# A decoder layer with three branches on one core: memory weights split two halves ahead, sums of x a step ahead, and three queue orders changed

## The chip, the core and the metric

The kernel runs on one core of a Trainium2 chip. Five engines work side by side, each on its own queue of instructions: TensorE (PE in the profile; PEld is its loading of the stationary operand), VectorE (DVE), ScalarE (ACT), GpSimd (POOL) and SyncE (SP). Here SP only issues DMAs, and its queue takes them in order: an issue that has to wait holds everything behind it. GpSimd issues a few DMAs too.

The metric is the device time of one execution in microseconds (us). A profiled execution also has a span, from its first to its last recorded instruction.

## The reference

One step of a decoder layer with 1024 prompt tokens and 8 sample tokens, width 1024, all in float32:

```python
mkv = mem_prompt @ w_mem_kv                 # 256 memory tokens, 2 x 1024 columns
mk, mv = mkv[:, :, 0], mkv[:, :, 1]         # memory keys and values, both outputs too
z = x @ w_in                                # xr, yr, q, k, v, xq, gates
a_out = rg_lru(causal_conv(xr)) * gelu(yr)  # branch a
s_out = sliding_window_attention(q, k, v)   # branch s, window 128
c_out = mem_attn(xq, mk, mv)                # branch c
merged = sum(gates[n] * (br @ w_branch[n]) for n, br in enumerate((a_out, s_out, c_out)))
h = layer_norm(ALPHA * x + merged @ w_out)
gt, up = split(h @ w_gate_up)
y = layer_norm(ALPHA * h + (silu(gt) * up) @ w_down)
```

For the sample tokens the kernel also returns the two window caches, shifted by one row and with the new row at the end (`s_win_k`, `s_win_v`; in the kernel `o_swk`, `o_swv`).

## The kernel before

**Products.** Every matrix product is made of float32 operands that are split in two: `split` (L71) has ScalarE cast a tile to fp32r (the high part, L73) and VectorE subtract that from the source (the low part, L74). A product of two split tiles is three TensorE instructions, high by high, high by low, low by high (`mm3`, L107 to L109). In the names of the trace `_h`, `H` or a leading `h` is a high part, `_l`, `L` or `l` a low part.

**Weights.** `half_raw` (L82, load L84) brings half a block of weights, 128 x 512, into one of six staging buffers by a DMA on SP; `half_pair` (L87) gives its split parts one of five buffers for the high and four for the low part. `weights` (L91) does both for a whole block.

**Stages**, in order of time:
- `mem_kv` (L360): the keys and the values of the 256 memory tokens. `memT`, the memory, comes in four halves (`mem_raw`, `mem_split`). Eight key blocks `m` follow, each of two weight halves with 12 matmuls; then four value groups `h` of four halves with 12 matmuls each. `put` (L366) evicts a finished block from PSUM with a ScalarE copy (L368) into one of two staging buffers (`kvraw`) and stores it twice by GpSimd DMAs, as an output and as scratch for branch c.
- `project` (L265): z = x @ w_in, in 30 units. A unit is two blocks of 128 columns, computed by a scheme of seven products of half size instead of eight (`fast_step`, steps 0 to 6, 24 matmuls each). It needs seven sums and differences of quarters of x (`combos`, L157; VectorE makes them at L177, L180, L181 and L190 and each is split; there are 14, for seven steps and two halves `p` of the tokens) and seven of each unit's weights (`fast_quarter`, sums at L205). PSUM tiles of a unit are called `ub`, `ud`, `uc`; `u2s` is an eviction of `ub` (L246). A unit ends in `Finish.done` (L1175), which for the twelve gate units stores the two results `za` and `zb` into scratch `scr_g` (L1181).
- The attention of branch c over the memory and of branch s over the window, with the projections of branch a (`branch(0, "a")`) and c filled in between. `load_branch` (L118) brings a branch's input back from scratch: eight loads (L124) per chunk of tokens, into the tiles that later hold the low parts (`baL`), and splits them. `dec_win_scores` (L824) handles the window attention of the sample tokens, and at L834 issues two copies inside DRAM, from `cwk` and `cwv` to `o_swk` and `o_swv` (127 rows for each of 8 tokens).
- The output product and `ffn` (L1053): 22 blocks `f`, for each the weights `wfg` and `wfu` and per chunk of tokens two products `fg` and `fu`, the multiplication of the two (L1064) and the split of the result `gH`; between them the products `d` with `wdn`.

**What sets the order.** The instructions are written down once, for all engines. For `mem_kv` and the first six steps (`FIRST`) of the first unit `tc.manual_schedule` (L290) keeps the written order on SP, ScalarE, VectorE and TensorE. [...] `tc.issue_after(x)` and `add_manual_dep` put an instruction behind another in that order without a wait on the chip.

In `mem_kv` before, the order inside one key block is: for each half the split of that half, the load of the same half of the next block, 12 products; then a load of a quarter of x, for four of the blocks one step of `moving` (the `combos` generator), and the eviction of this very block. A value group loads and splits each half directly ahead of its products. `moving` makes a sum and splits it in the same step. After `mem_kv` come the loads of unit 0, three quarters of its weights, and per step of the first six one quarter and two steps of `moving`.

## Time and profile before

| what | value |
|---|---|
| median of three runs | 2045.55 us (2042.29 to 2048.28) |
| profiled execution | 2043.52 us, its span 2041.8 us |
| granted TensorE clock, mean | 0.988 |
| TensorE busy | 1974.8 us, 97% of the span |
| VectorE busy | 1199.2 us, 59% |
| ScalarE busy | 876.0 us, 43% |
| GpSimd busy | 126.1 us, 6% |
| DMA | 239.62 MB, 117 GB/s in the mean |

How to read it: the profile cuts the span in 40 slices and gives each engine's busy share in tenths (9 is 90% or more). A row of a single instruction has its start in us, its duration in us, engine, line of the kernel, operation, the tiles it writes and reads, shapes and types, and in brackets the idle time ahead of it with what ended that. A row of the waits names the group that waited, what released it, the total of the wait in us, the number of waits and the longest. A group's row has its line, engine, operation, tiles, count, then minimum, median and maximum in ns and the stretch in which it lies. A row of DMAs has the number of transfers, KB of each and the median us from issue to landing; an issuing row has the duration on the queue. The clock is the share of full speed that TensorE was granted.

### The profile page before, as it was taken

The numbers are of one execution on the slowest core, as the hardware profiler recorded it, in microseconds if no ns is written. First come the engines' busy times: TensorE is split into PE (matmuls) and PEld (weight loads), VectorE is DVE, ScalarE is ACT, GpSimd is POOL, SyncE is SP. The second block draws the span as 40 slices with busy tenths as digits, with TensorE's granted clock in tenths as the row PEclk, the third lists the DMA queues.
The fourth block names the chain that finished last, engine by engine and source line by source line (L and its number), as shares of the span: only waits on it lengthen the run. The fifth ranks groups of instructions, "written<-read, shape, count | busy, mean of one in ns | idle before, by whom it ended". The sixth has DMA issues, their size and how long they took to land.

```text
span 2041.8 us, 35429 instructions
## 1 busy us (share of the span) xinstructions
PE 1974.8 (97%) x13732; PEld 1937.0 (95%) x13732; DVE 1199.2 (59%) x2561; ACT 876.0 (43%) x1914; POOL 126.1 (6%) x192
## 2 busy tenths in 40 slices
PE   6799999999999988999999999999999999999997
PEld 5799999999999987988999999999999999999996
DVE  5678888977766654378876558623322232223357
ACT  4446655564655544378774244422111221122224
POOL 1200001010000000011110002100000000000001
PEclk9899999999999998999999999999999999999999
DMA  7455554546223366667525241111111111111112
GB/s 274 145 171 169 188 174 157 166 148 225 103 94 126 121 233 207 206 169 208 162 81 174 83 150 38 37 46 42 52 52 42 42 50 46 51 52 42 52 32 83
DMA packets 140824, 239.62 MB, mean 117 GB/s; under 512 B 17664, under 2 KB 67920, under 8 KB 140624
## 3 DMA queue, kind: packets, MB, share of 16 engines
q1 hardware_dynamic: 139120, 233.17, 35.6%
q0 software_dynamic: 1536, 4.20, 0.6%
q8 instruction: 108, 1.77, 0.4%
q14 instruction: 60, 0.49, 0.1%
HBM read 182.05 MB, written 57.33 MB: 117 GB/s over the span
## 4 chain that ended last, share of the span: by engine, by line
PE 87%; DVE 4%; ACT 4%; DMA 3%; issue 1%; SPq 0%; ACTq 0%; POOL 0%; DVEq 0%; POOLq 0%
PE ub L223 5%; PE ub L222 5%; PE ub L221 5%; PE fg L107 4%; PE fg L108 4%; PE fg L109 4%; PE fu L109 4%; PE fu L107 4%; PE fu L108 4%; PE d L107 3%; PE d L109 3%; PE d L108 3%; PE ud L223 3%; PE ud L222 3%; PE ud L221 3%; PE brs L107 1%
## 5 line engine op out<-in xcount | busy, mean ns | idle before, releaser
L107 PE MATMUL fg<-hH,wfg_h 128*128 128x384 f32 (+1 forms) x528 | 168.2, 319 | 2.9 <-DVE acc L1035 1.7
L108 PE MATMUL fg<-hL,wfg_h 128*128 128x384 f32 (+1 forms) x528 | 167.7, 318 | 0.4 <-DVE hL L1046 0.4
L109 PE MATMUL fu<-hH,wfu_l 128*128 128x384 f32 (+1 forms) x528 | 167.7, 318 | 0.0
L108 PE MATMUL fu<-hL,wfu_h 128*128 128x384 f32 (+1 forms) x528 | 167.6, 317 | 0.0
L107 PE MATMUL fu<-hH,wfu_h 128*128 128x384 f32 (+1 forms) x528 | 167.5, 318 | 0.0
L109 PE MATMUL fg<-hH,wfg_l 128*128 128x384 f32 (+1 forms) x528 | 167.5, 317 | 0.0
L1064 DVE TENSOR_TENSOR ft<-ft,fu 128x384 f32<-128x384 f32 (+1 forms) x66 | 33.8, 513 | 139.2 <-PE fu L109 139.1
L107 PE MATMUL d<-gH,wd_h 128*128 128x384 f32 (+1 forms) x360 | 114.4, 318 | 0.0
L108 PE MATMUL d<-gL,wd_h 128*128 128x384 f32 (+1 forms) x360 | 114.2, 317 | 0.0
L109 PE MATMUL d<-gH,wd_l 128*128 128x384 f32 (+1 forms) x360 | 114.2, 317 | 0.0
L1062 DVE SCALAR_TENSOR_TENSOR ft<-ft,fg 128x384 f32<-128x384 f32 (+1 forms) x66 | 33.8, 512 | 135.4 <-ACT ft L1061 133.2
L73 ACT CAST gH<-ft 128x384 fp32r<-128x384 f32 (+1 forms) x66 | 31.7, 480 | 174.8 <-DVE ft L1064 174.7
L107 PEld LDWEIGHTS fg<-hH,wfg_h 128*128 128x128 f32 x528 | 99.1, 188 | 3.9 <-DVE acc L1035 2.0
L108 PEld LDWEIGHTS fg<-hL,wfg_h 128*128 128x128 f32 x528 | 99.2, 188 | 1.0 <-DVE hL L1046 0.9
L109 PEld LDWEIGHTS fg<-hH,wfg_l 128*128 128x128 f32 x528 | 99.2, 188 | 0.0
L109 PEld LDWEIGHTS fu<-hH,wfu_l 128*128 128x128 f32 x528 | 99.2, 188 | 0.0
L107 PEld LDWEIGHTS fu<-hH,wfu_h 128*128 128x128 f32 x528 | 99.2, 188 | 0.0
L108 PEld LDWEIGHTS fu<-hL,wfu_h 128*128 128x128 f32 x528 | 99.1, 188 | 0.0
L1084 DVE SCALAR_TENSOR_TENSOR acc<-d,acc 128x384 f32<-128x384 f32 (+1 forms) x48 | 24.8, 516 | 108.4 <-PE d L109 108.4
L1061 ACT ACTIVATE ft<-fg 128x384 f32<-128x384 f32 (+1 forms) x66 | 30.1, 456 | 135.1 <-PE fg L109 135.1
L221 PE MATMUL ub<-th,u_4h 128*128 128x258 f32 x240 | 68.7, 286 | 5.8 <-ACT u2s L246 5.8
L556 ACT ACTIVATE bp<-bp,bst 128x257 f32<-128x257 f32 (+1 forms) x128 | 62.8, 493 | 18.8 <-DVE bst L552 18.6
(937 smaller groups left out, 6885.7 us busy)
## 6 DMA issues: line engine op xcount, KB each, us to landing
ur<-win SPq DMA_DIRECT2D x120, 256.0 KB, 2.8
dck<-cmk SPq DMA_DIRECT2D x32, 256.0 KB, 2.9
dcv<-cmvT SPq DMA_DIRECT2D x32, 256.0 KB, 3.1
st<-scr_q SPq DMA_DIRECT2D x32, 256.0 KB, 4.4
scr_g<-za SPq DMA_DIRECT2D x12, 516.0 KB, 2.8
scr_g<-zb SPq DMA_DIRECT2D x12, 516.0 KB, 3.9
x<-xQ SPq DMA_DIRECT2D x8, 516.0 KB, 6.0
scr_a<-ge SPq DMA_DIRECT2D x8, 516.0 KB, 2.8
```

The lines of the kernel that those rows point to most:

```text
L73: ins = self.nc.scalar.copy(hi, src).ins
L107: nc.tensor.matmul(ps, sh, mh, start=opens and i == 0, stop=False)
L108: nc.tensor.matmul(ps, sh, ml, start=False, stop=False)
L109: self.last_mm = nc.tensor.matmul(ps, sl, mh, start=False, stop=closes and i == last).ins
L221: mm(sh[:, w], xh, start=opens and k == 0, stop=False)
L222: mm(sh[:, w], xl, start=False, stop=False)
L223: self.last_mm = mm(sl[:, w], xh, start=False, stop=k == 3).ins
L556: nc.scalar.activation(x, x, AF.Exp, bias=st[:, g:g + 1], scale=-1.0, accum_out=st[:, 4 + g:5 + g])
L1061: nc.scalar.activation(t, pg, AF.Tanh, scale=0.5)
L1062: nc.vector.scalar_tensor_tensor(t, t, 1.0, pg, op0=ALU.add, op1=ALU.mult)
L1064: nc.vector.tensor_mul(t, t, pu)
L1084: nc.vector.scalar_tensor_tensor(a, ps, 0.5, a, op0=ALU.mult, op1=ALU.add)
```

## The change

- **Memory stage.** The 16 key halves and 16 value halves become one loop over 32 halves `n`. The load of a half is issued four halves ahead of its products (`fetch`), its split two halves ahead (`cut`), and the eviction of a finished block or group comes one half after its last product, in the next block's time. 24 matmuls on a constant tile (`WARM`) are put ahead of everything on TensorE. The loads of unit 0 and its first quarters are issued in the loop's last iterations.
- **Sums of x.** `combos` makes the sum for the next step ahead of the split for this one, and yields the number of VectorE operations; the memory loop takes a step whenever its count `due` allows one. The first six steps take two steps of `moving` each for k < 3 and one after that.
- **Branch a.** The eight loads of its first chunk depend, in order alone, on `last_gate`, the store of the last gate unit's `zb`: that store is queued behind them.
- **Cache copies.** The two copies inside DRAM move from `dec_win_scores` to the FFN, behind the weight loads of the blocks f = 2 and f = 4.

```diff
+WARM = 24
...
-            self.nc.sync.dma_start(lo.bitcast(F32), self.scr[br][:, k, t0:t0 + n])
+            ins = self.nc.sync.dma_start(lo.bitcast(F32), self.scr[br][:, k, t0:t0 + n]).ins
+            if br == "a" and c == 0:
+                self.tc.add_manual_dep(self.last_gate, ins.name, mybir.DependencyInfo(
+                    mybir.DependencyClass.NoSync, mybir.DependencyReason.DATA), reason="order of the queue")
...
-        for i in range(7):
-            for p in range(2):
-                b11, b12, b22, b21 = (xs.get((f, p)) for f in ((0, 0), (0, 1), (1, 1), (1, 0)))
-                if i == 0:
-                    keep(0, p, b11)
-                elif i == 1:
-                    t1 = self.zt(f"t1_{p}")
-                    tt(t1, b11, b12, ALU.subtract)
-                    keep(1, p, t1)
-                elif i == 2:
-                    tt(b12, b22, b12, ALU.subtract)
-                    tt(b11, b12, b11, ALU.add)
-                    keep(2, p, b11, -1.0)
-                elif i == 3:
-                    keep(3, p, b21)
-                elif i == 4:
-                    keep(4, p, b12)
-                elif i == 5:
-                    keep(5, p, b22)
-                else:
-                    tt(b11, b11, b21, ALU.subtract)
-                    keep(6, p, b11)
-                yield
+        def make(i, p):
+            b11, b12, b22, b21 = (xs.get((f, p)) for f in ((0, 0), (0, 1), (1, 1), (1, 0)))
+            if i == 1:
+                t1[p] = self.zt(f"t1_{p}")
+                tt(t1[p], b11, b12, ALU.subtract)
+                return 1
+            if i == 2:
+                tt(b12, b22, b12, ALU.subtract)
+                tt(b11, b12, b11, ALU.add)
+                return 2
+            if i == 6:
+                tt(b11, b11, b21, ALU.subtract)
+                return 1
+            return 0
+
+        steps = [(i, p) for i in range(7) for p in range(2)]
+        for n, (i, p) in enumerate(steps):
+            cost = 1
+            if n + 1 < len(steps):
+                cost += make(*steps[n + 1])
+            src = {0: xs[(0, 0), p], 1: t1.get(p), 2: xs[(0, 0), p], 3: xs.get(((1, 0), p)), 4: xs.get(((0, 1), p)),
+                   5: xs.get(((1, 1), p)), 6: xs[(0, 0), p]}[i]
+            keep(i, p, src, -1.0 if i == 2 else 1.0)
+            yield cost
...
-                self.mem_kv(moving, xs)
-            load(0)
-            for u, i in todo[:ahead]:
-                self.fast_quarter(st[u], i)
+                self.mem_kv(moving, xs, lambda: load(0), [lambda i=i: self.fast_quarter(st[0], i) for i in range(2)])
+            self.fast_quarter(st[0], 2)
             for k, (u, i) in enumerate(todo[:FIRST]):
                 if i == 1:
                     load(u + 1)
                 v, j = todo[k + ahead]
                 self.fast_quarter(st[v], j)
-                for _ in range(2):
+                for _ in range(2 if k < 3 else 1):
...
-            ps = self.bank("mm", f"mk{m}")[:, :NM]
-            for e in range(2):
-                hi, lo = self.half_pair(f"wmk{m}_{e}")
-                self.split(hi, lo, raws.pop((m, e)))
-                if m + 1 < KT:
-                    raws[m + 1, e] = key_half(m + 1, e)
-                for k in range(4 * e, 4 * e + 4):
-                    if k >= len(memx):
-                        mem_split(mraw[k // 2])
-                    w = slice(k % 4 * P, (k % 4 + 1) * P)
-                    self.mm3(ps, [((hi[:, w], lo[:, w]), memx[k])], k == 7, k == 0)
-            (f, th), p = quarters[m]
-            xs[(f, th), p] = self.x_quarter(f, th, p)
-            if m >= 2:
-                if m in (2, 3, 5, 7):
-                    next(moving)
-            put(ps, io["o_pmk"][:, m, :], "mk", m)
...
+        def fetch(n):
+            if n < 16:
+                src = io["wmk"][n // 2][:, n % 2 * h:(n % 2 + 1) * h]
+            else:
+                src = io["wmv"][(n - 16) // 2][:, n % 2 * h:(n % 2 + 1) * h]
+            raws[n] = self.half_raw(src, h, f"wm{n}r")
+
+        def cut(n):
+            pairs[n] = self.half_pair(f"wm{n}_")
+            self.split(*pairs[n], raws.pop(n))
+
+        def key(n):
+            m, e = n // 2, n % 2
+            if e == 0:
+                sums[m] = self.bank("mm", f"mk{m}")[:, :NM]
+            hi, lo = pairs.pop(n)
+            cols = [slice(i * P, (i + 1) * P) for i in range(4)]
+            self.mm3(sums[m], [((hi[:, w], lo[:, w]), memx[4 * e + i]) for i, w in enumerate(cols)], e == 1, e == 0)
+
+        def value(n):
+            g, j = (n - 16) // 4, n % 4
+            if j == 0:
+                sums[g] = [self.bank("mm", f"mv{g}_{tt}")[:, :256] for tt in range(2)]
+            hi, lo = pairs.pop(n)
+            cols = [slice(i * 256, (i + 1) * 256) for i in range(2)]
+            for tt in range(2):
+                xs_ = [tuple(a[:, tt * P:(tt + 1) * P] for a in memx[2 * j + i]) for i in range(2)]
+                self.mm3(sums[g][tt], [(x, (hi[:, w], lo[:, w])) for x, w in zip(xs_, cols)], j == 3, j == 0)
+
+        warm = self.bank("o", "warm")
+        for _ in range(WARM):
+            nc.tensor.matmul(warm[:, :P], self.ones, self.ones, start=True, stop=True)
+        for f in (partial(mem_raw, 0), partial(fetch, 0), partial(mem_raw, 1), partial(mem_raw, 2), partial(fetch, 1),
+                  partial(mem_raw, 3), partial(fetch, 2), partial(fetch, 3)):
+            f()
+        for f in (partial(mem_split, 0), partial(cut, 0), partial(mem_split, 1), partial(mem_split, 2), partial(cut, 1),
+                  partial(mem_split, 3)):
+            f()
+        due = -3.5
+        for n in range(32):
+            if n + 4 < 32:
+                fetch(n + 4)
+            elif n == 28:
+                load()
+            if n % 2 == 0 and n < 16:
+                (f, th), p = order[n // 2]
+                xs[(f, th), p] = self.x_quarter(f, th, p)
+            if n + 2 < 32:
+                cut(n + 2)
+            else:
+                quarters[n - 30]()
+            due += 0.6
+            if due > 0:
+                due -= next(moving)
+            (key if n < 16 else value)(n)
+            if 0 < n <= 16 and n % 2 == 0:
+                put(sums.pop(n // 2 - 1), io["o_pmk"][:, n // 2 - 1, :], "mk", n // 2 - 1)
+            if n > 16 and n % 4 == 0:
+                g = (n - 16) // 4 - 1
+                for tt, ps in enumerate(sums.pop(g)):
+                    put(ps, io["o_pmv"][:, tt, g * 256:(g + 1) * 256], "mv", 2 * g + tt)
+        for tt, ps in enumerate(sums.pop(3)):
+            put(ps, io["o_pmv"][:, tt, 768:], "mv", 6 + tt)
...
-        for name, cache, row in (("o_swk", "cwk", krow), ("o_swv", "cwv", self.vd)):
-            with self.tc.issue_after(self.last_load):
-                nc.sync.dma_start(io[name][:, 0:P - 1, :], io[cache][:, 1:P, :])
+        for name, row in (("o_swk", krow), ("o_swv", self.vd)):
...
+                if f in (2, 4):
+                    name, cache = (("o_swk", "cwk"), ("o_swv", "cwv"))[f // 2 - 1]
+                    with self.tc.issue_after(self.last_load):
+                        nc.sync.dma_start(io[name][:, 0:P - 1, :], io[cache][:, 1:P, :])
...
-                nc.sync.dma_start(b.scr["g"][:, 2 * j + e, :], z)
+                b.last_gate = nc.sync.dma_start(b.scr["g"][:, 2 * j + e, :], z).ins
```

More of the change, by code (lines that the diff above doesn't have):

```diff
@@ L160, in combos @@
         tt = self.nc.vector.tensor_tensor
+        t1 = {}
         def keep(i, p, src, sign=1.0):
@@ L358, in v_rows, with mem_kv @@
             yield
-    def mem_kv(self, moving, xs):
+    def mem_kv(self, moving, xs, load, quarters):
         nc, io = self.nc, self.io
-        memx = []
+        h = D // 2
+        memx, raws, pairs, sums = [], {}, {}, {}
+        order = [(f, p) for f in ((0, 0), (0, 1), (1, 1), (1, 0)) for p in range(2)]
         def put(ps, out, name, m):
@@ L379, in mem_split @@
             for i in range(2):
-                k = len(memx)
-                memx.append(tuple(self.ph.tile([P, NM], F32R, tag="mem", name=f"mem{e}{k}", bufs=16) for e in "hl"))
-                self.split(*memx[k], raw[:, i * NM:(i + 1) * NM])
-        quarters = [(f, p) for f in ((0, 0), (0, 1), (1, 1), (1, 0)) for p in range(2)]
-        raws = {}
-        mraw = [mem_raw(0)]
-        raws[0, 0] = key_half(0, 0)
-        mraw.append(mem_raw(1))
-        raws[0, 1] = key_half(0, 1)
-        mraw += [mem_raw(2), mem_raw(3)]
@@ L410, in mem_kv @@
-        for h in range(4):
-            pv = [self.bank("mm", f"mv{h}_{tt}")[:, :256] for tt in range(2)]
-            for j in range(4):
-                raw = self.half_raw(io["wmv"][2 * h + j // 2][:, (j % 2) * 512:(j % 2 + 1) * 512], 512, f"wmv{h}_{j}r")
-                wh, wl = self.half_pair(f"wmv{h}_{j}")
-                self.split(wh, wl, raw)
-                for tt in range(2):
-                    for i in range(2):
-                        xh, xl = (a[:, tt * P:(tt + 1) * P] for a in memx[2 * j + i])
-                        vh, vl = (a[:, i * 256:(i + 1) * 256] for a in (wh, wl))
-                        nc.tensor.matmul(pv[tt], xh, vh, start=j + i == 0, stop=False)
-                        nc.tensor.matmul(pv[tt], xh, vl, start=False, stop=False)
-                        self.last_mm = nc.tensor.matmul(pv[tt], xl, vh, start=False, stop=j + i == 4).ins
-                if j == 2 or (j == 1 and h >= 2):
-                    next(moving)
-            for tt, ps in enumerate(pv):
-                put(ps, io["o_pmv"][:, tt, h * 256:(h + 1) * 256], "mv", 2 * h + tt)
+                memx.append(tuple(self.ph.tile([P, NM], F32R, tag="mem", name=f"mem{e}{2 * k + i}", bufs=16)
+                                  for e in "hl"))
```

11 lines of the change are left out of this document (5 added, 6 removed).

## The prediction

> **What bounds the kernel now.** I read the page first, then the busy time by stretches, the waits of TensorE, the timelines of the stretches that stand out, and the DMA rates there.
>
> ```profile
> span 2041.8 us, 35429 instructions
> ```
> ```profile
> PE   6799999999999988999999999999999999999997
> ```
>
> The second line is TensorE's busy share in tenths, in 40 slices of 51 us. It is full nearly everywhere; it is not in the first two slices and has a dent at slices 15 and 16 (715 to 816 us). The FFN, 9s to the end, has nothing to give. A gain must come from those two places.
>
> ```profile
> 0.00:51.00 51.00, 34.29 (x229) 30.46 (x229) 25.80 (x39) 22.60 (x42) 9.02 (x20) 1.00 0.77 274
> 51.00:102.00 51.00, 38.73 (x262) 36.26 (x262) 33.54 (x55) 24.69 (x45) 10.27 (x24) 0.84 0.45 145
> 102.00:153.00 51.00, 51.00 (x419) 50.96 (x419) 40.57 (x106) 24.13 (x49) 0.92 (x2) 0.99 0.51 171
> ```
> ```profile
> PE mk L107 <- ACT wmk_0h L73: 12.7, 8, 5.6
> PE ub L221 <- ACT u2s L246: 5.8, 1, 5.8
> ```
>
> The columns of the first fence: stretch, its length, busy us of PE, PEld, DVE, ACT, POOL, clock, DMA share, GB/s. TensorE lacks 16.7 and 12.3 us there, and nothing from 102 us on. The waits name ScalarE: casts of the memory weights and evictions, although ScalarE is busy under half the time. So it is late by order, not by load:
>
> ```profile
> 15.58 0.28 PE L109 MATMUL mk<-memh,wmk_1l 128*128 128x256 f32 x1
> 15.90 0.37 ACT L368 COPY mkr<-mk 128x256 f32<-128x256 f32 x1 [3.16 <-PE mk L109]
> 16.17 0.62 ACT L73 CAST wmk_0h<-wmk_0r 128x512 fp32r<-128x512 f32 x1
> ```
> ```profile
> 33.14 1.06 ACT L73 CAST th<-t 128x1032 fp32r<-128x1032 f32 x1 [1.98 <-DVE t L177]
> ```
> ```profile
> L74 DVE TENSOR_TENSOR tl<-x,th x2: 1235/1235/1235, 18.3 to 22.9; 128x1032 fp32r<-128x1032 f32 x2
> L177 DVE TENSOR_TENSOR t<-x,x x2: 1224/1225/1226, 31.9 to 41.2; 128x1032 f32<-128x1032 f32 x2
> ```
>
> ScalarE's queue holds the eviction of a key block (15.90) ahead of the cast of the next block's weights (16.17). The eviction waits for TensorE's last product (15.58), TensorE for the cast: the eight blocks cost it the 12.7 us of the first wait. The cast of a sum (33.14) waits 1.98 us in the same queue for a sum that VectorE has just begun; a sum takes 1.22 us there and a split's low part 1.23 (min, median, max in ns).
>
> **The change, part by part.** *A, the memory stage and the first unit.* Cuts now stand two half blocks ahead and the eviction one iteration behind, so the eviction finds its product done and two cut halves lie between TensorE and a stall. What TensorE alone needs:
>
> ```profile
> 5.65 0.58 PE L107 MATMUL mk<-memh,wmk_0h 128*128 128x256 f32 x1 [5.65 <-ACT wmk_0h L73]
> ```
> ```profile
> 45.67 0.28 PE L422 MATMUL mv<-wmv_0h,meml 128*128 128x256 f32 x1
> ```
> ```profile
> 49.52 0.28 PE L422 MATMUL mv<-wmv_2h,meml 128*128 128x256 f32 x1
> ```
> ```profile
> 104.30 0.28 PE L221 MATMUL ud<-th,u_5h 128*128 128x258 f32 x1
> ```
>
> 33 steps from 45.67 to 49.52 are 0.1167 us each; in the steady stretch above, 51.00 us for 419 products are 0.122. The 32 half blocks of 12 products take 44.8 us, steps 0 to 4 of the first unit (120 products) 14.6. From the first product at 5.65 step 5 (ud) could start at 65.1; it starts at 104.30. Bound: 39.2 us.
>
> The loads forbid part of that. Up to the twentieth weight half (n=19, issued behind the last quarter of x) the SP queue must bring 4 halves of mem and 20 of weights at 0.262 MB and 8 quarters of x at 0.528; about 8 blocks of stores (2 x 0.131 MB each) share the engines: 6.3 + 4.2 + 2.0 = 12.5 MB.
>
> ```profile
> x<-xQ SPq DMA_DIRECT2D x8, 516.0 KB, 6.0
> ```
> ```profile
> mem<-memT SPq DMA_DIRECT2D x4, 256.0 KB, 4.4
> o_pmk<-mkr POOLq DMA_DIRECT2D x8, 128.0 KB, 4.2
> ```
> ```profile
> 0.00:5.00 5.00, 0.00 (x0) 0.00 (x0) 0.54 (x4) 1.94 (x4) 0.19 (x4) 1.00 0.49 162
> 5.00:11.30 6.30, 5.64 (x24) 5.22 (x24) 4.03 (x10) 3.27 (x9) 0.00 (x0) 1.00 0.94 292
> 11.30:16.00 4.70, 3.37 (x24) 2.96 (x24) 1.29 (x2) 1.51 (x4) 1.31 (x2) 1.00 0.98 353
> 16.00:20.50 4.50, 3.38 (x24) 2.96 (x24) 2.53 (x3) 2.26 (x4) 1.07 (x2) 1.00 1.04 414
> 20.50:25.10 4.60, 3.37 (x24) 2.96 (x24) 2.53 (x3) 2.36 (x4) 1.07 (x2) 1.00 1.03 389
> ```
>
> Length times rate: 0.81, 1.84, 1.66, 1.86, 1.79, so 7.96 MB by 25.1 us, with the engines full (share 0.94 and more) from 5 us on even now. The last three full rows make 385 GB/s. The other 4.5 MB take 11.8 us: half 19 lands at 36.9 and is cut 1.1 us later, so its product starts at 38.0, where TensorE alone would be at 32.3. Behind it loads are light (a half per 0.7 us against 1.4 of products). There VectorE decides once: n=19 brings two sums and a split, 1.22 + 1.22 + 1.23 us, where a half leaves it 1.4, and the third cut ahead is late by some 1.2. Thirteen halves of 1.40 end at 57.4. The first unit has 14.6 us of products against some 12 of VectorE work (four splits 4.9, two sums 2.4, seven half as wide 4.3), part of it begun before; its 5.8 us wait (second wait above) came from sums made in line, now a step ahead, so I cost it at nothing; without that cover it is 5.8 again. Step 5 starts at 72.0: **A = -32.3**. Bounds: -39.2 if loads hold nothing back; if the rest flows at 292 GB/s, the second row's rate, 15.4 us in place of 11.8, and half of the 5.8 stays, -26.
>
> [...]
>
> The 24 warm-up products (ones by ones, 128 wide) sit on an empty TensorE ahead of 5.65. Such products are in no row; the nearest are the 256 wide ones, 0.117 per step, so 24 x 0.117 = 2.8 us at most, done before the data; any speed-up of the first halves is swallowed by the wait for half 19. I cost them at nothing. If each took 0.58, as the cold row at 5.65, they would last 13.9 us and, with 19 halves of 1.40 behind them, cost 2.5.
>
> *B, branch a's first loads.*
>
> ```profile
> 724.58 0.34 SPq L1181 DMA_DIRECT2D scr_g<-za  x1
> 726.76 0.33 SPq L1181 DMA_DIRECT2D scr_g<-zb  x1
> 727.18 4.13 SPq L124 DMA_DIRECT2D baL<-scr_a  x8
> ```
> ```profile
> 730.87 0.69 PE L107 MATMUL bra<-baH,wba_h 128*128 128x384 f32 x1 [5.09 <-ACT baH L73]
> ```
>
> The eight loads stand behind the store of zb, which waits for TensorE's last product of the stage; TensorE then idles 5.09 us and follows the loads to the eighth. Ahead of that store they come behind the store of za, at 724.92: 2.26 us earlier, and the chain with them. The zb store goes some 2 us later than now (724.92 and the eight issues, 4.13), and behind it only the gate loads, needed when the first block is evicted, after its 24 products. **B = -2.3**; nothing if another waiting load comes between; -7 (the 5.09, and about 2 for the cold start: 0.69 in that row) if the planner puts the loads ahead of za too.
>
> *C, the copies leave the attention stage.*
>
> ```profile
> 770.00:780.00 10.00, 6.81 (x32) 4.45 (x31) 2.58 (x5) 4.14 (x8) 0.37 (x2) 1.00 0.63 203
> 780.00:790.00 10.00, 8.57 (x48) 7.94 (x47) 1.57 (x3) 0.56 (x2) 1.48 (x6) 0.66 0.66 196
> 790.00:800.00 10.00, 8.94 (x50) 8.29 (x50) 7.25 (x22) 6.70 (x23) 0.00 (x0) 0.83 0.93 309
> ```
> ```profile
> 748.51 0.72 SPq L834 DMA_DIRECT2D o_swv<-cwv  x1
> 753.45 0.32 SPq L634 DMA_DIRECT2D gta<-scr_g  x1
> 770.30 2.68 SPq L490 DMA_DIRECT2D scr_c<-cob  x2
> ```
>
> Behind the copy at 748.51 the planner's order has one load and then, for 16.5 us, nothing; the next loads stand behind a store of results (770.30). I read this as the planner booking a copy inside DRAM as long and ordering late everything that follows. TensorE loses 3.2 + 1.4 + 1.1 us in these rows, and the clock (0.66, 0.83) about 5 more. Without the copy the order should be closer to the chip's. **C = -5**, half of what is lost; bounds -11 and, since any new order can hold a load up, +3.
>
> *D, the copies arrive in the FFN.* They stand ahead of the loads of blocks 3 and 5.
>
> ```profile
> 1347.26 0.62 ACT L73 CAST wfg_h<-wfg4r__16993 128x512 fp32r<-128x512 f32 x1 [0.84 <-PE fu L108]
> 1347.84 0.41 ACT L73 CAST gH<-ft 128x264 fp32r<-128x264 f32 x1
> ```
> ```profile
> 1347.38 0.43 DVE L1064 TENSOR_TENSOR ft<-ft,fu 128x264 f32<-128x264 f32 x1 [0.77 <-PE fu L109]
> ```
> ```profile
> 1304.31 0.33 SPq L84 DMA_DIRECT2D wfg3r__16795<-wgu  x1
> ```
>
> Now a weight half is cast up to a block ahead. If the planner believes those weights late, it puts their cast behind the block's last eviction (1347.84): TensorE waits for that product's multiplication, 0.43, the eviction, 0.41, the cast, 0.62 as above, and the low part: about 2 us per copy. **D = +4**. Below: 0, if the planner keeps the order. Above: +9 with the clock lost twice.
>
> ```profile
> 52.04 0.58 PE L421 MATMUL mv<-wmv_3l,memh 128*128 128x256 f32 x1 [0.98 <-DVE wmv_3l L74]
> ```
>
> Here, after a wait of 0.98 us with another shortly before, a product takes 0.58 in place of 0.28. [...]
>
> **Sum:** -32.3 - 2.3 - 5 + 4 = -35.6. The profiled execution took 2043.5 us (the span, and 1.7 around it), which gives 2007.9; the median of the runs shown, 2045.55, is 2.0 above it, so 2009.9. I give 2009.
>
> **The rivals.** *The loads do not bind* (0.18): A is -39, 2003. For it: single rows reach 414 GB/s; against: the engines are already full. *The wait moves to VectorE and ScalarE* (0.20): VectorE has ten splits (12.3), six sums (7.3) and 32 low parts at half a split's 1.23 (19.7), 39 us in 45 of products, and takes them in order; an eviction needs one of two staging buffers, free when a store of 4.2 us (median) has landed, and holds the cuts behind it. Half of the 16 evictions losing 1 us: 2017. *The edits of order do nothing* (0.05): B and C zero, because loads still queue behind a waiting instruction: 2017 with D, 2021 if the FFN loses its clock. *The copies hold the FFN's weights* (0.02): the slower side. If a copy kept the queue for longer than the 43 us between the issue of block 3's first weights (1304.31) and their use after 1347.26, each further us would cost one, twice; with 39.6 us gained elsewhere the kernel is slower from about 63 us per copy; at 68, 2056. Against it: the load at 753.45 went out 5 us after a copy.
>
> **How the numbers follow.** The forecast has 0.55, its own range 2002 to 2016. The range 1998 to 2022 takes in the three next cases and the bounds of A; what is left out are the last rival and the ends of several terms at once. 0.3% (6 us) is about what a measurement of this kernel can tell from no change: faster 0.95, same 0.03, slower 0.02.
>
> **What would show it.** Step 5 of the first unit at 72 (65: loads did not bind; over 80: the wait moved; the waits then name who). TensorE's waits in the key blocks on weights landing, not on ScalarE behind an eviction; DMA share near 1 until about 37 us. The loads of branch a issued right behind the za store, and an idle of about 2.8 us. Fewer idle us between 765 and 800 of now. Two gaps of 2 us in the FFN at blocks 3 and 5. If step 5 does not move, the prediction is wrong at its root.

## The result and the profile after

The changed kernel takes 2013.89 us (median of four runs, 2012.51 to 2015.44), the kernel before 2044.15 beside it: a ratio of 0.9849, 95% interval 0.9832 to 0.9867. The prediction was 2009 with 1998 to 2022. The profiled execution took 2013.65, its span first in this fence of the page, then TensorE's busy share in 40 slices of 50 us.

```profile
span 2011.6 us, 35485 instructions
...
PE   8999999999999999999999999999999999999997
```

The first slice is at 8 in place of 6, and the dents at the second slice and at slices 15 and 16 are gone. The stretches of the start, as before (columns: stretch, length, busy us of PE, PEld, DVE, ACT, POOL, clock, DMA share, GB/s):

```profile
0.00:51.00 51.00, 45.52 (x330) 43.82 (x331) 35.40 (x51) 30.70 (x57) 12.86 (x28) 1.00 0.89 319
51.00:102.00 51.00, 46.94 (x367) 46.25 (x367) 40.95 (x90) 26.67 (x53) 6.49 (x17) 0.93 0.55 182
```

TensorE lacks 5.5 and 4.1 us there in place of 16.7 and 12.3 (5.4 of the busy time are the warm-up products, 24 of 0.22 us, where the prediction had 2.8 us at most for them). What it waits for up to 140 us, in the view of the waits, and three starts from its timeline (half 19, unit 0, step 5 of unit 0):

```profile
PE ub L228 <- ACT u2s L253: 3.4, 1, 3.4
PE mv L109 <- DVE wm_l L75: 2.1, 2, 1.4
PE mk L110 <- DVE wm_l L75: 1.8, 4, 1.2
```
```profile
40.96 0.28 PE L108 MATMUL mv<-wm_h,memh 128*128 128x256 f32 x1
60.56 0.28 PE L228 MATMUL ub<-th,u_0h 128*128 128x258 f32 x1
81.92 0.36 PE L228 MATMUL ud<-th,u_5h 128*128 128x258 f32 x1
```

Both traces hold the same 13732 products (the warm-up left out), so the start of the n-th can be set against the n-th. This table is worked out from all of TensorE's rows:

| product | what starts there | before, us | after, us | after less before |
|---|---|---|---|---|
| 228 | half 19 of the memory weights | 50.67 | 40.96 | -9.7 |
| 384 | unit 0 | 81.19 | 60.56 | -20.6 |
| 504 | step 5 of unit 0 | 104.30 | 81.92 | -22.4 |
| 5600 | last step of the last unit | 725.38 | 705.15 | -20.2 |
| 5800 | in the attention, behind the first projection of branch a | 762.66 | 743.14 | -19.5 |
| 6000 | in the attention, behind the old place of the copies | 806.23 | 775.12 | -31.1 |
| 6760 | in the window attention | 931.19 | 896.30 | -34.9 |
| 9380 | end of FFN block 2 | 1346.45 | 1312.05 | -34.4 |
| 9690 | in FFN block 5 | 1394.93 | 1364.80 | -30.1 |
| last | | 2028.56 | 1998.41 | -30.2 |

So in this pair of traces the order edits gave nothing at branch a (-20.2 to -19.5), much where the copies were (-11.6), and cost 4.3 where they went. The -3.8 from product 6000 to 6760 is taken up with the last run; the rest is the start.

**The copies' old place and new place.** Stretches of 10 us around products 5800 to 6000, changed kernel:

```profile
740.00:750.00 10.00, 10.00 (x74) 9.78 (x73) 7.04 (x19) 5.40 (x17) 0.00 (x0) 1.00 0.89 291
750.00:760.00 10.00, 10.00 (x74) 9.24 (x72) 4.75 (x11) 4.72 (x13) 1.02 (x5) 1.00 0.69 222
760.00:770.00 10.00, 9.17 (x54) 7.68 (x53) 5.46 (x17) 5.56 (x18) 0.19 (x1) 1.00 0.79 246
```

0.8 us lost in 30 and the clock at 1.00, where before 5.7 us were idle and the clock fell to 0.66. In the FFN, the chain of one gap in the timelines of ScalarE and TensorE:

```profile
1313.44 0.41 ACT L74 CAST gH<-ft 128x264 fp32r<-128x264 f32 x1 [2.93 <-DVE ft L1088]
1313.75 0.61 ACT L74 CAST wfg_h<-wfg3r__16819 128x512 fp32r<-128x512 f32 x1
1314.42 0.45 PE L108 MATMUL fg<-hH,wfg_h 128*128 128x384 f32 x1 [1.48 <-ACT wfg_h L74]
```

The cast of block 3's weights stands behind the block's last eviction (1313.44), though those weights were issued 42 us earlier; TensorE waits 1.48 us, and the start of the next block slips by 2.1. In the kernel before, the first of these casts starts at 1324.77, ahead of block 1's last eviction (1325.36). Both kernels write it behind block 2's products and differ there by the copy alone, so the FFN's queues do not hold the written order. What orders them is called the planner here; how it chooses, no run shows.

### The profile page after: what moved, and what is told of

It reads as the page before. It is cut to its first block, busy times and chain, and to the rows that moved or that the text cites. A ratio compares the mean times of both kernels' runs of the same rounds, so it can differ in the third digit from the quotient of the medians.

```text
span 2011.6 us, 35485 instructions
## 1 busy us (share of the span) xinstructions
PE 1966.9 (98%) x13756; PEld 1934.2 (96%) x13756; DVE 1197.2 (60%) x2561; ACT 875.4 (44%) x1914; POOL 128.1 (6%) x192
## 4 chain that ended last, share of the span: by engine, by line
PE 85%; DVE 6%; DMA 4%; ACT 4%; issue 1%; SPq 0%; ACTq 0%; POOL 0%; DVEq 0%
PE ub L230 5%; PE ub L228 5%; PE ub L229 5%; PE fg L110 4%; PE fg L108 4%; PE fg L109 4%; PE fu L110 4%; PE fu L108 4%; PE fu L109 4%; PE d L108 3%; PE d L109 3%; PE d L110 3%; PE ud L230 2%; PE ud L229 2%; PE ud L228 2%; PE brs L108 1%
## 5 line engine op out<-in xcount | busy, mean ns | idle before, releaser
L1085 ACT ACTIVATE ft<-fg 128x384 f32<-128x384 f32 (+1 forms) x66 | 30.1, 456 | 138.1 <-PE fg L110 138.1
L228 PE MATMUL ub<-th,u_0h 128*128 128x258 f32 x240 | 68.3, 285 | 3.0 <-ACT zb L1201 2.4
```

Of the source, the lines that this page charges most:

```text
L228: mm(sh[:, w], xh, start=opens and k == 0, stop=False)
L1085: nc.scalar.activation(t, pg, AF.Tanh, scale=0.5)
```

## The experiments

All are timed against the kernel before on the same chip. This table sets out the stretches of every trace, in us, worked out like the one above: starts of half 19 and unit 0; from unit 0 to its step 5; TensorE's idle ahead of branch a; from the last product of the projections to 78 products into branch a (B); products 5800 to 6000 (C); 9380 to 9690 (D).

| run | median | half 19 | unit 0 | to step 5 | idle | B | C | D |
|---|---|---|---|---|---|---|---|---|
| before | 2044.15 | 50.67 | 81.19 | 23.11 | 5.09 | 21.3 | 43.6 | 48.5 |
| e12_before_again | 2043.57 (one run) | 49.82 | 79.23 | 23.07 | 5.08 | 21.3 | 44.0 | 48.5 |
| changed | 2013.89 | 40.96 | 60.56 | 21.36 | 4.98 | 22.0 | 32.0 | 52.8 |
| e3_copies_back | 2018.60 | 40.99 | 60.21 | 21.23 | 2.90 | 19.9 | 45.0 | 48.5 |
| e9_memory_alone | 2019.09 | 40.03 | 59.56 | 20.31 | 5.11 | 21.0 | 44.0 | 48.5 |
| e4_gate_back | 2010.14 | 40.14 | 59.51 | 21.40 | 3.42 + 1.32 | 22.0 | 32.6 | 52.8 |
| e5_tail | 2006.62 | 40.03 | 58.91 | 20.61 | 4.61 | 21.0 | 32.1 | 48.5 |
| e2_spread | 2008.06 | 40.23 | 59.21 | 16.05 | 3.81 | 19.8 | 32.1 | 55.9 |
| e1_staging | 2010.64 | 39.60 | 59.30 | 19.66 | 4.92 | 22.0 | 32.2 | 52.8 |
| e6_unpile | 2006.37 | 40.70 | 61.84 | 15.38 | 3.80 | 19.9 | 32.0 | 52.8 |
| e7_half_stores | 2008.76 | 38.65 | 56.85 | 20.37 | 3.51 | 19.3 | 32.4 | 54.3 |
| e8_nowarm | 2012.33 | 39.80 | 58.87 | 19.57 | 3.58 | 19.7 | 32.1 | 54.3 |
| e10_best | 1999.05 | 40.61 | 59.95 | 15.42 | 3.87 | 20.3 | 32.5 | 48.5 |
| e11_best_za | 2002.83 | 40.70 | 59.36 | 15.48 | 1.91 | 18.3 | 33.5 | 48.5 |

Rows with the same order in a stretch show what repeats: unit 0 starts between 58.9 and 60.6 in the six traces with the changed memory stage untouched. The projections, from step 5 to the last unit, took 620.6 to 624.9 us over the fourteen traces, and 621.2 and 623.9 in the two of the kernel before: a single pair can't tell 4 us there. The totals differ between sets as well: e1 and e4 lie 3.2 and 3.8 us under the changed kernel, and neither edit shows a gain clear of the spread of the same stretches in other traces. So a difference of 4 us between two medians is not read as an edit's here.

### The copies and the order at branch a

**e3_copies_back**

```diff
-        for name, row in (("o_swk", krow), ("o_swv", self.vd)):
+        for name, cache, row in (("o_swk", "cwk", krow), ("o_swv", "cwv", self.vd)):
+            with self.tc.issue_after(self.last_load):
+                nc.sync.dma_start(io[name][:, 0:P - 1, :], io[cache][:, 1:P, :])
...
-                if f in (2, 4):
-                    name, cache = (("o_swk", "cwk"), ("o_swv", "cwv"))[f // 2 - 1]
-                    with self.tc.issue_after(self.last_load):
-                        nc.sync.dma_start(io[name][:, 0:P - 1, :], io[cache][:, 1:P, :])
```

> The changed kernel with the two copies inside DRAM back in the attention stage. Theory P (the planner books them as long and orders late what follows; the move took about 15 us off the stretch behind the window scores and put 4.3 into the FFN): the stalls and the low clock 45 to 80 us behind the first product of branch a come back, the two gaps of 2.1 us in the FFN go, and the kernel takes 2022 to 2026. Rival (most of the 15 us came from where the clock happened to drop): the waits come back with about 6 us, the clock stays at 0.95 or more, and the kernel takes 2013 to 2017.

It takes 2018.60 (ratio 0.9881, 0.9864 to 0.9897), 4.7 above the changed kernel: between the range of theory P and that of the rival. By the stretches theory P holds: C is 45.0 in place of 32.0, the two FFN gaps are gone (48.5), and the waits and the low clock are back (windows of this run):

```profile
745.00:755.00 10.00, 8.10 (x40) 5.33 (x39) 3.32 (x5) 4.15 (x8) 0.06 (x1) 1.00 0.23 82
755.00:765.00 10.00, 7.80 (x39) 6.73 (x38) 1.39 (x2) 1.62 (x3) 1.44 (x6) 0.74 0.68 200
765.00:775.00 10.00, 9.04 (x40) 8.30 (x40) 3.74 (x14) 2.85 (x12) 0.37 (x2) 0.50 0.89 275
```

5.1 us idle, and a clock of 0.74 and 0.50 behind it. The queue of SP shows the order that does it, the second copy and the next issue behind it:

```profile
733.24 0.72 SPq L860 DMA_DIRECT2D o_swv<-cwv  x1
749.72 2.67 SPq L516 DMA_DIRECT2D scr_c<-cob  x2
```

The copy holds the queue for 0.72 us, and then nothing is issued for 15.8 us, much as in the kernel before; the DMA engines are at 0.26 from 734 to 750 us, so it is not the copy's bytes that delay the loads. (That the planner books the copy as long is the author's reading of this order; no run shows what it reckons with.) The rival (clock stays up, 6 us) is out: the move is worth 12 to 13 us there and costs 4.3. What the total lacks against that lies outside: the idle ahead of branch a was only 2.90 us here, and the median of the four runs is 2.7 under the profiled one (2021.28).

**e4_gate_back**

```diff
-            if br == "a" and c == 0:
+            if False:
```

> The changed kernel without the order of branch a's first loads ahead of the last gate store. Theory G (the lead of 2.3 us is given back: the loads share the engines with the store of za and the first lands 5.2 us after its issue in place of 3.1, so TensorE's idle is 4.98 against 5.09): the idle ahead of the first product of branch a is 5.0 to 5.2 us, and the kernel is within 1.5 us of 2013.9. Rival (the prediction's term of 2.3 is there and a longer cold clock hides it): the idle is 7 us or more, and the kernel takes about 2016.

2010.14 (0.9839, 0.9822 to 0.9855): not slower than with the edit, so the rival is out. It lies 3.8 under the changed kernel, which theory G didn't expect either; the stretch B is 22.0 in both traces, and they differ by 1.0 in all, at the start, so this is not the edit's. The idle is 4.7 us where theory G had 5.0 to 5.2, and in two parts, 3.42 and 1.32, since the planner by itself put one of the eight loads ahead of the store: the run takes back seven eighths of the edit.

Where the lead went can be read in rows of the changed kernel's SP queue, ScalarE and TensorE, and in the same of e3:

```profile
703.76 0.33 SPq L85 DMA_DIRECT2D wba4r__10994<-wbr  x1
704.35 0.33 SPq L1209 DMA_DIRECT2D scr_g<-za  x1
704.77 4.49 SPq L125 DMA_DIRECT2D baL<-scr_a  x8
709.96 4.04 ACT L74 CAST baH<-baL 128x384 fp32r<-128x384 f32 x8 [3.45 <-DMA baL<-scr_a]
710.53 0.69 PE L108 MATMUL bra<-baH,wba_h 128*128 128x384 f32 x1 [4.98 <-ACT baH L74]
```
```profile
705.84 4.12 SPq L125 DMA_DIRECT2D baL<-scr_a  x8
708.94 1.02 ACT L74 CAST baH<-baL 128x384 fp32r<-128x384 f32 x2 [1.37 <-DMA baL<-scr_a]
709.50 0.69 PE L108 MATMUL bra<-baH,wba_h 128*128 128x384 f32 x1 [2.90 <-ACT baH L74]
```

In the changed kernel the loads go out 0.5 us ahead of the last product (705.27), as predicted, but a weight half and the store of za, 0.8 MB together, were issued within the microsecond ahead of them, and the first cast starts 5.2 us after the issue. In e3, where the planner had no weights right there, it starts 3.1 us after, and the idle is 2.9, near the 2.8 us that the prediction named.

These bytes are not the whole cause. In e1, e2, e5 to e8 and e10 the same weight half and store stand ahead of the loads at the same distances, and there the first cast starts 3.7 to 5.1 us after the issue and the idle is 3.5 to 4.9. So the two transfers go with at least 0.6 us, and why the rest differs between traces of the same order stays open. The clock adds to it: by the traces' clock records TensorE gets half its clock around that place for 3.41 us in four of the eight traces, with a B of 19.3 to 19.9, and for 6.83 us in the other four, with 20.3 to 22.0. One pair of traces tells little of this edit.

**e9_memory_alone** is e3 with the edit of e4 too, so that the memory stage and the sums alone are new.

> The kernel before with the memory stage and the sums of x of the changed one alone: copies in the attention stage, the last gate store ahead of branch a's loads. Against the run with the copies back (2018.6, idle of 2.90 us ahead of branch a, the same planner's order ahead of the loads but for the store), this gives the third edit by itself. Theory B (it is worth what the prediction gave it, 2.2, where no weights stand ahead of the loads): the idle is about 5.1 us again, the stretch from the last product to 78 products into branch a about 21.3 in place of 19.85, and the kernel takes about 2020.5. Rival (the lead is worth nothing there either): the idle is under 3.5 us, the kernel within 1.5 us of 2018.6.

2019.09 (0.9885, 0.9868 to 0.9901). The idle is 5.11 again and B 21.0: theory B by the stretches, with 1.2 of the 2.2 left once the low clock is counted. By the total the two kernels can't be told apart (0.5). The run also gives the first two parts of the change by themselves: 24.3 us under the kernel before (2043.41 beside it).

**e5_tail**

```diff
-                if f in (2, 4):
...
                     w[m] = self.resident(io["wdn"][m][:, f0 * P:(f0 + nf) * P], nf, f"wdl{m}", 0)
+                    if m == KT - 1:
+                        for name, cache in (("o_swk", "cwk"), ("o_swv", "cwv")):
+                            with self.tc.issue_after(self.last_load):
+                                nc.sync.dma_start(io[name][:, 0:P - 1, :], io[cache][:, 1:P, :])
```

> The changed kernel with the two copies inside DRAM behind the last weight load of the FFN in place of the second and fourth block. Theory P (a copy only hurts because the planner books it as long and orders late what is loaded behind it; nothing is loaded behind these): the gaps ahead of the FFN's blocks 3 and 5 go (the stretch over both 48.5 us in place of 52.75), no new one comes, and the kernel takes about 2009.6. Rival (the copies themselves disturb the loads or the last stores on the chip): a wait of the same size shows in the last 100 us, and the kernel is within 1.5 us of 2013.9.

2006.62 (0.9813, 0.9799 to 0.9828). 100 us of the FFN without and with the gap, this run first, then the changed kernel:

```profile
1340.00:1440.00 100.00, 100.00 (x643) 100.00 (x642) 31.35 (x57) 21.41 (x41) 0.00 (x0) 1.00 0.17 48
```
```profile
1350.00:1450.00 100.00, 98.41 (x633) 97.88 (x632) 30.80 (x56) 21.11 (x41) 0.00 (x0) 1.00 0.16 48
```

D is 48.48, and from product 9690 to the end it takes the same 633.6 us: no new wait. The total is 7.3 under the changed kernel where theory P had 4.3; in the trace 4.3 lie in D and 2.4 ahead of step 5, which the edit doesn't touch. The gap comes with the copy's place in the program. That it is the planner's order and not late data is in the row of 1313.75 above: it names no wait, so the cast only took its turn behind the eviction.

### The first unit

**e2_spread**

```diff
-                for _ in range(2 if k < 3 else 1):
+                for _ in range(1):
```

> The changed kernel with one step of the sums of x per product step in the first unit, in place of two for the first three. Theory V (the eviction u2s stood behind a cast that stood behind VectorE's pile of two sums and four low parts in two steps): the wait of 3.42 us ahead of step 4 and the cold clock behind it (24 products in 5.3 us where 2.9 would do) go, step 5 starts at about 76 in place of 81.9, and the kernel takes about 2008. Rival (VectorE is full and the pile only moves): a wait of 2 us or more turns up ahead of step 5 or 6, and the kernel is within 1.5 us of 2013.9.

2008.06 (0.9826, 0.9809 to 0.9843). The changed kernel's rows ahead of step 4, VectorE and ScalarE, then the same in e2:

```profile
71.38 1.23 DVE L187 TENSOR_TENSOR x<-x,x 128x1032 f32<-128x1032 f32 x1
72.52 2.44 DVE L75 TENSOR_TENSOR tl<-x,th 128x1032 fp32r<-128x1032 f32 x2
74.88 0.68 DVE L212 TENSOR_TENSOR us<-us,ur 128x512 f32<-128x512 f32 x1
75.65 0.62 ACT L74 CAST u_5h<-us 128x512 fp32r<-128x512 f32 x1 [1.41 <-DVE us L212]
76.18 0.64 ACT L253 COPY u2s<-ub 128x258 f32<-128x258 f32 x2
76.60 0.58 PE L228 MATMUL ub<-th,u_4h 128*128 128x258 f32 x1 [3.42 <-ACT u2s L253]
```
```profile
69.60 0.68 DVE L212 TENSOR_TENSOR us<-us,ur 128x512 f32<-128x512 f32 x1
70.38 0.62 ACT L74 CAST u_5h<-us 128x512 fp32r<-128x512 f32 x1 [2.20 <-DVE us L212]
71.86 0.64 ACT L253 COPY u2s<-ub 128x258 f32<-128x258 f32 x2
72.28 0.39 PE L228 MATMUL ub<-th,u_4h 128*128 128x258 f32 x1 [0.95 <-ACT u2s L253]
```

In the first, the sum for the weights of step 5 (74.88) stands behind a sum and two low parts of x, the cast behind that sum, the eviction u2s behind the cast, and TensorE behind the eviction: 3.42 us, and then 24 products at 0.22 us each, 5.3 in place of 2.9. With one step of the sums per product step the sum starts at 69.60, the wait is 0.95, and the 24 products of step 4 take 3.0 us. From unit 0 to step 5 it takes 16.1 us in place of 21.4; no wait of 2 us turned up behind it. Theory V. (The medians differ by 5.8. In this trace B is 2.2 shorter than in the changed kernel's, and the FFN's two gaps cost 7.4 in place of 4.3, with the clock at 0.98 over 200 us there.)

### The memory stage

**e1_staging**

```diff
-            raw = self.sm.tile([P, 256], F32, tag="kvraw", name=f"{name}r{m}", bufs=2)
+            pool, bufs = ((self.sm, 2), (self.ph, 3))[m % 5 > 1]
+            raw = pool.tile([P, 256], F32, tag="kvraw", name=f"{name}r{m}", bufs=bufs)
```

> The changed kernel with five staging buffers for evicted memory keys and values in place of two. Theory S (the casts wait behind evictions that wait for a staging buffer: ScalarE lost 11.4 us to stores landing, and TensorE some 5 us of its 9.5 in the memory stage): unit 0 starts at 55.5 to 57 us in place of 60.56, and the kernel takes about 2010. Theory L (the prediction: the loads bind up to half 19): half 19 starts where it did, at about 41 us, unit 0 at 59.5 or later, and the kernel is within 1.5 us of 2013.9.

2010.64 (0.9842, 0.9826 to 0.9858). Unit 0 starts at 59.30, within what the unchanged stage does (58.9 to 60.6), and not at 55.5 to 57: theory S falls, although ScalarE no longer waits for the stores. Theory L's total (within 1.5 of 2013.9) was missed as well, by the difference between sets named above. ScalarE's rows for half 19, changed kernel, then e1:

```profile
39.13 0.38 ACT L376 COPY mkr<-mk 128x256 f32<-128x256 f32 x1 [2.46 <-DMA scr_mk<-mkr]
39.40 0.62 ACT L74 CAST wm_h<-wm19r 128x512 fp32r<-128x512 f32 x1
```
```profile
37.87 0.62 ACT L74 CAST wm_h<-wm19r 128x512 fp32r<-128x512 f32 x1 [2.54 <-DMA wm19r<-wmv]
```

In the changed kernel the eviction waits 2.46 us for a store and the cast follows it; with five buffers the cast waits 2.54 us for its own load. One wait hides the other: half 19 landed at about 37.8 (the prediction had 36.9), and its product starts at 39.6. It does not wait for its own cast there, which is done at 38.5: half 17 is late, in e1 and in the changed kernel. Two VectorE rows of the changed kernel, the first sum of a pile and the low part behind it:

```profile
33.84 1.23 DVE L183 TENSOR_TENSOR x<-x,x 128x1032 f32<-128x1032 f32 x1
37.40 0.68 DVE L75 TENSOR_TENSOR wm_l<-wm17r,wm_h 128x512 fp32r<-128x512 f32 x1
```

**e6_unpile**

```diff
...
+                yield 1
                 tt(b11, b12, b11, ALU.add)
-                return 2
+                yield 1
...
-            cost = 1
             if n + 1 < len(steps):
-                cost += make(*steps[n + 1])
+                yield from make(*steps[n + 1])
...
-            yield cost
+            yield 1
...
-                for _ in range(2 if k < 3 else 1):
+                for _ in range(2 if k == 0 else 1):
```

> The changed kernel with the sums of x dealt out one VectorE operation at a time: a step of the generator is one sum or one split, in the memory stage at the same mean rate, in the first unit two steps at product step 0 and one at each later one. Theory V (the piles of two sums and a low part, 3.7 us in one half of 1.4, hold the low part of a weight half, with TensorE waiting 2.0 to 2.3 us at halves 17 and 18 and about 1 at half 23; and the pile in the first unit costs about 6): unit 0 starts at 56.5 to 58 (59.2 to 60.6 in the four runs so far), step 5 at 72 to 74, and the kernel takes about 2006. Rival (the loads alone set the memory stage): unit 0 starts at 59 or later, step 5 at 75 to 76, the kernel about 2008.

2006.37 (0.9814, 0.9799 to 0.9829), but not by the memory stage: the first unit takes 15.4 to step 5, and B is 2.1 shorter. In the memory stage theory V was wrong, and unit 0 starts even later than the rival had it, at 61.84. TensorE's waits on VectorE at halves 17 and 18 fell to 0.2 us, and this came in their place (the SP queue's waits from 15 to 40 us, and ScalarE's timeline):

```profile
SPq L158 <- DVE tl L75: 4.0, 1, 4.0
```
```profile
40.03 0.62 ACT L74 CAST wm_h<-wm19r 128x512 fp32r<-128x512 f32 x1 [2.83 <-DMA wm19r<-wmv]
```

With the splits of x dealt out later, the last quarter of x waits 4.0 us for its tile (1.2 in the changed kernel) and holds the weight halves behind it in the queue; half 19 lands at 40.0 in place of 37.8. So this run takes away the pile and delays the loads at once; it doesn't test the pile alone.

**e7_half_stores**

```diff
-            nc.gpsimd.dma_start(out, raw)
```

(on top of e1; it leaves out two of the outputs, so its 2008.76 is not the time of a whole kernel)

> The kernel with five staging buffers, and without the stores of the memory keys and values to the two outputs (these two outputs are left out; the stores to scratch stay). Theory L (the DMA engines bind up to half 19): about 1 MB less is moved by then, at 400 GB/s 2.6 us, so half 19 starts at 37 to 38 in place of 39.6, unit 0 at about 57 in place of 59.3. Rival (VectorE's pile, not the loads): half 19 starts at 39 to 40, unit 0 at 59 or later.

Half 19's cast, and TensorE's wait for the low part of half 17 behind the pile of sums:

```profile
35.43 0.62 ACT L74 CAST wm_h<-wm19r 128x512 fp32r<-128x512 f32 x1 [0.91 <-DMA wm19r<-wmv]
35.86 0.39 PE L109 MATMUL mv<-wm_l,memh 128*128 128x256 f32 x1 [1.18 <-DVE wm_l L75]
```

Half 19 lands at 35.4, 2.4 earlier, where 2.6 was expected of 1 MB less: the loads do go at the rate of full engines (share 1.03 to 1.04, 400 to 409 GB/s from 20 to 35 us in this run). But its product starts only 0.95 earlier, at 38.65, because VectorE's pile of two sums and a low part (33.84 to 37.4 in the changed kernel) holds half 17 all the same. Behind that nothing waits any more: 13 halves take 18.2 us, TensorE's own time, and unit 0 starts at 56.85. Loads and pile are two limits within a microsecond or two: with the loads earlier the pile remains, and where e6 spread the pile the loads came later.

**e8_nowarm**

```diff
-WARM = 24
+WARM = 0
```

> The changed kernel without the 24 warm-up products. The prediction costs them at nothing: the first product starts at about 5.65 in place of 6.22, the first half takes about 3 us in place of 2.67, half 19 starts at 40 to 41 as with them, and the kernel is within 1.5 us of 2013.9. Rival (they keep the clock up for the first halves): half 4 starts 2 us or more later, unit 0 at 62 or later, the kernel at 2016 or more.

2012.33 (0.9843, 0.9828 to 0.9858): the warm-up products are worth nothing that can be measured. The first product starts at 5.69, half 4 at 13.90 (13.95 with them).

### Put together

**e10_best** joins e1, e2 and e5; **e11_best_za** adds branch a's loads ahead of both gate stores:

```diff
...
-                self.tc.add_manual_dep(self.last_gate, ins.name, mybir.DependencyInfo(
-                    mybir.DependencyClass.NoSync, mybir.DependencyReason.DATA), reason="order of the queue")
+                for store in self.last_gate:
+                    self.tc.add_manual_dep(store, ins.name, mybir.DependencyInfo(
+                        mybir.DependencyClass.NoSync, mybir.DependencyReason.DATA), reason="order of the queue")
...
```

> The changed kernel with five staging buffers, one step of the sums of x per product step in the first unit, and the copies behind the FFN's last weight load. If the gains add (about 6 in the first unit, 1 from the staging buffers, 4.3 in the FFN, and what the clock gives or takes): step 5 starts at 74 to 75.5, the FFN stretch over blocks 3 and 5 is 48.5, and the kernel takes 1999 to 2003. If the first unit's gain is taken back by the next wait behind it, it takes 2005 or more.

> The same kernel with branch a's first loads ahead of both last gate stores, not of the second alone. Theory G (the lead is lost to the store of 0.53 MB and the weights issued right ahead of the loads: the first of them lands 5.2 us after its issue in the changed kernel, 3.1 where no weights stand ahead): the idle ahead of branch a is 2.5 to 3.2 us in place of 4 to 5, and the kernel is 1 to 2.5 us under the one beside it. Rival (the weights ahead alone hold it): the idle stays over 4 us, no difference of 1 us.

e10 takes 1999.05 (0.9786, 0.9771 to 0.9800), 14.8 under the changed kernel and the fastest here; step 5 starts at 75.37 and D is 48.5. e11 takes 2002.83 (0.9805, 0.9790 to 0.9819). Its idle ahead of branch a is down to 1.91 and B to 18.3, as theory G has it and more; the first cast starts 2.7 us after the issue with a weight half alone right ahead, so the rival (the weights alone hold it) is out. Yet it is slower than e10. Its trace is 2.9 us longer in the projections, where both have the same order, and 1.0 and 2.0 longer in the two stretches of the attention behind B, where the planner's order differs. How much of the 3.8 the edit causes stays open.

**e12_before_again**

> The kernel before once more, for what one trace of it leaves open: whether its stretches repeat. Step 5 of unit 0 at 103 to 105.5, the stretch of the copies 43 to 44.5 us (32 in the changed kernel). The stretch behind it, 125.0 in the first trace and 120.8 to 122.8 in all eight others: if it is 124 or more again, it belongs to the order before; if it is 121 to 122.5, the 3.8 us were a drop of the clock in that one execution.

Step 5 starts at 102.3 and C takes 44.0. Products 6000 to 6760 took 122.7 us against 125.0 in the first trace, at the upper end of the other twelve (120.8 to 122.9): more than half of the 3.8 us that the pair of traces gave there belongs to one execution.

## Why the prediction held, and where it was off

The forecast was -35.6; the medians say -30.3. By its own terms, with the mean over the traces that share the order in place of one pair:

| term | predicted | bounds given | measured | from |
|---|---|---|---|---|
| A, start to step 5 | -32.3 | -39..-26 | -22.6 | 5 traces, 80.7, against 103.3 |
| B, branch a's first loads | -2.3 | -7..0 | -0.7 | 8 traces, 20.5, against 21.2 in 3 |
| C, copies leave the attention | -5 | -11..+3 | -11.9 | 9 traces, 32.2, against 44.1 in 4 |
| D, copies enter the FFN | +4 | 0..+9 | +4.3, or 5.8 to 7.4 where the clock drops too | 4 and 3 traces against 48.5 |

The sum of the measured terms is -30.9. A by itself can be read from e9 too: -24.3 by the medians.

**A fell outside its bounds, and the step that failed is the first unit's.** Step 5 started at 81.92, in the part (over 80) where the prediction had said that the wait has moved. The prediction cost its wait for u2s "at nothing", because sums now come a step ahead, and said that without the cover it is 5.8 again. The sums did come ahead, but six VectorE operations on x were still packed into the first two product steps, and the chain sum, cast, eviction, product stayed. The first unit took 21.4 us to step 5 where the prediction had 14.6: 6.8 of the 9.9 us missing. e2 took 5.3 of them back with one number changed. VectorE's work was undercounted as well: the prediction has seven operations of half width, the trace has four sums and seven low parts of the weights for this unit, and VectorE is busy 13.6 of the 16.0 us from unit 0 to step 4.

The other 3.2 came ahead of unit 0, which was due at 57.4 and started at 60.56 (58.9 to 60.6). Half 19 landed 0.9 later than worked out (e1), a size. The other part is a wait that the prediction had not seen: it counts one pile of two sums and a split, behind half 19, at 1.2 us. The changed kernel has two, from 33.84 and from 41.87 on, and the first stands ahead of half 17's low part, so that half 19 started late for half 17's sake and not for its own load. Behind half 19 the forecast held: 19.6 us to unit 0, where 19.4 was worked out. The DMA rows bear out the rate (share 1.03 to 1.05 and 401 to 414 GB/s from 16 to 35 us). The rival "the loads do not bind" is out by e7: with 1 MB less to move unit 0 starts at 56.85 in place of e1's 59.30. The rival "the wait moves to VectorE and ScalarE" was partly right, in the pile and in the first unit; its price for the two staging buffers was wrong (e1). The warm-up products took 5.38 us, more than the prediction's "2.8 us at most", because they ran at 0.22 us each; that they are worth nothing held (e8).

**C was mis-sized on the good side.** The reading, that the planner books a copy inside DRAM as long and orders late what follows, held as far as the order goes: with the copies back the hole in the queue (15.8 us) and the stall (5.1 us idle, a clock of 0.74 and 0.50) are back. That the planner books durations at all, which this term and D's rest on, no run shows; the runs show where copies and casts stand in the queues, and what TensorE waits for. The prediction took half of what is lost because a new order might hold something else up. It held nothing up, and the whole loss went, waits and low clock, a little past the bound of 11. The rival "the edits of order do nothing" is out by this.

**D was right in mechanism and size**: the cast behind the block's last eviction, 2.1 us per copy. The cast's row shows that it is a matter of order and not of data, and e5 that the gap goes when the copies do. In three of the seven traces with these gaps (e2, e7, e8) the clock halves behind a wait of 1.48 us (D of 54.3 to 55.9 in place of 52.8; a mean clock of 0.98 over 200 us in e2), as the prediction's upper bound allowed. The rival "the copies hold the FFN's weights" is out: both together cost 4.3.

**B was right as a mechanism where its condition held** (idle of 2.9 in e3, 5.1 in e9) and mostly lost in the changed kernel, where the idle was 4.98. The prediction gave "nothing if another waiting load comes between"; no load came between, but a weight half and the store of za were issued right ahead, and the loads landed later. With the same order seven other traces idle 3.5 to 4.9 us, so that -0.7 is a mean over a wide spread.

The errors of A and C partly cancelled (+9.7 and -6.9), so the total was nearer than its parts; that part of the agreement is luck.

## What to carry to other kernels

Making work a step earlier does not help an engine that takes its queue in order if as much work is still packed ahead of the one sum that the next engine waits for: count the operations between the waiting instruction and the head of its queue, and spread them. A transfer can cost more through the order that a planner makes behind it (12 us here) than through the queue (0.7 us); put it where nothing is loaded behind it. When two limits lie close together (loads and a pile here), taking one away shows little, so test them together before calling either one harmless.

## What the runs showed of the hardware

The granted clock adds noise of its own. The same idle of 5 us ahead of branch a was followed by a stretch of slow products that ended at 734.59 in the kernel before, 3.7 us after its first product, and at 716.73 in the changed one, 6.2 us after:

```profile
734.59 0.36 PE L108 MATMUL bra<-baL,wba_h 128*128 128x384 f32 x1
```
```profile
716.73 0.45 PE L108 MATMUL bra<-baH,wba_h 128*128 128x384 f32 x1
```

By the clock records of the two traces the half clock lasts 6.83 us in both, from 727.79 and from 710.12 on; in the kernel before 3.1 us of it fall into the idle time, in the changed one 0.4.

The time until products run fast differs from run to run as well: the six traces with the changed memory stage untouched all start their first product at 6.22, and the first product of 0.28 to 0.30 us starts at 9.0 to 11.4. Why it differs, no run shows.

The warm-up did not warm. In the changed kernel TensorE is busy from 1.04 us on without a break:

```profile
1.04 5.38 PE L421 MATMUL warm<-ones 128*128 128x128 f32 x24 [1.04 <-DVE ones L142]
8.89 0.41 PE L108 MATMUL mk<-memh,wm_h 128*128 128x256 f32 x1
```

At 8.89 a product still takes 0.41 us, and the first at 0.28 to 0.30 starts at 10.38; over the eleven traces with the warm-up it starts at 8.4 to 11.4, over the three without it at 9.1 to 11.0. Counted from the first product on data, that is 2.2 to 5.2 us with the warm-up and 3.4 to 5.4 without. So 24 products of 128 by 128 over 5.4 us did not bring the fast ones: these came 7.4 to 10.4 us after the first of the 24.
